# Banded heads of a hybrid attention layer: the half-precision parts of the probabilities are made with queries on partitions and turned by transposing DMAs

## The chip, the cores and the metric

The kernel runs on one core of one Trainium2 chip. The metric is the device time of one execution in microseconds. Before the change it is 1192.52 us, the median of three runs (1192.51 to 1194.84).

## The reference

One decoder layer for one sequence of 2048 tokens and a width of 1024, with two kinds of attention heads side by side. Eight heads of width 64 are "forgetting" heads (causal softmax with a gate bias); eight are banded heads: each query attends to the 128 keys that end at itself, two key heads serve four query heads each, and a learned sink per head enters the softmax's sum only.

```python
h = rms_norm(x, g_pre) * (1 + scale) + shift
qa, ka, va, fa, za, qb, kb, vb, zb = split(h @ w_in)
oa = forgetting_attention(qa, ka, va, fa + b_fgate) * silu(za)
qb, kb = rope(qb), rope(kb)
# banded heads: a block of 128 queries sees its own 128 keys and the block before
s = einsum('bnqhgd,bnshd->bnhgqs', qb, with_prev(kb)) * d ** -0.5
s = where(band & valid, s, -inf)
p = softmax(concat([s, sink]))[..., :-1]
ob = einsum('bnhgqs,bnshd->bnqhgd', p, with_prev(vb)) * silu(zb)
y = concat([oa, ob]) @ w_out
out = x + gate * rms_norm(y, g_post)
```

## The kernel before, in words

Everything is float32 outside. Inside, a product is made of three float16 matmuls: each factor is split into a high part (its value rounded to float16) and a low part (the rest), and high by high, high by low and low by high are summed in PSUM. So wherever a result becomes a factor again, ScalarE (ACT) writes the high part with a copy and VectorE (DVE) the low part with a subtraction.

The program has four stretches: a prologue (modulation, normalisation, the transposed input, the projections of the banded keys and values; up to some 153 us), the banded heads (to some 424 us), the forgetting heads (to some 1020 us) and the output projection. The change lies in the second.

**The banded heads** are 32 windows of class `Pair`: four pairs of heads `j`, and for each the 16 query blocks two by two. One window has two heads and two blocks, so four score tiles of 128 queries by up to 256 keys; the first block of the sequence has no block ahead of it, so four of the 32 windows have six tiles of 128x128 instead of eight. The steps of a window:

- `scores` (L839): twelve matmuls into a PSUM tile `pss`, queries on partitions.
- `maxima` (L852, L856): a fused VectorE instruction per tile adds the band mask, writes the masked scores to `sm_` in SBUF and gives the row maximum; one more makes the bias of the exponential. `sm_` has one extra column per tile for the sink.
- `exps` (L863): four ScalarE exponentials in place in `sm_`, each with its row sum.
- `turn` (L872): TensorE transposes the eight tiles, in float32, into the PSUM tile `pxb`. At the next tick ScalarE copies `pxb` to the high part in `ptb` (L881), at the tick behind it VectorE makes the low part from `pxb` (L877) and the reciprocals of the row sums (L879).
- `pv` (L891): 24 matmuls with keys on partitions; the factors are the tiles of `ptb` and the values `vb`. One tick later VectorE scales the result by the reciprocals into `on` (L897), and a GpSimd DMA stores it (L899).

`sm_`, `ptb`, `pss`, `pxb` and the result `pob` have one buffer each.

**What else runs in this stretch.** TensorE fills the time between these steps with projection units (`fill`): L316 for queries, keys and gates, L334 for values of the forgetting heads, into three PSUM banks `bk`. What follows a unit on the other engines is delayed by ticks. Query projections of the banded heads go through the rotary step: ScalarE copies the bank (L704), four DMAs on SP's queue swap the halves (L706), VectorE multiplies by the cosine (L709), GpSimd by the sine (L719), VectorE adds (L720), ScalarE writes the high part (L721) and VectorE the low part `stb` (L713). Gates have L364, L366 and L356, values L339 and L343. Weights of coming units are loaded, their scale is found on VectorE and GpSimd (L206 to L246), and they are split (L254, L260). Beside it pieces of the output weight are loaded on SP's queue (`wsq`, L1107) and their squares summed on ScalarE (L1103), one piece per window.

**What sets the order.** The instructions of this stretch stand on each engine's queue in the order in which the program emits them (`tc.manual_schedule`), with no scheduler behind it. `tick()` emits what was delayed until then by `after(n, f)`. One window is: a tick; `maxima(n)`; a quarter of the units; a tick; `exps(n)`; a quarter; a tick; a quarter; a tick; a quarter; `pv(n-1)`; `turn(n)`; `scores(n+1)`; the square of piece n-2 and the load of piece n. So the part of `turn` on the other engines is emitted in the window after.

Of the kernel before, what the change touches and what calls it, by code (L numbers as in the profile page):

```python
# [23 lines left out]
CH = 512  # L24
# [16 lines left out]
def hybrid_layer(  # L41
# [17 lines left out]
    V, A, G, PE, SP = nc.vector, nc.scalar, nc.gpsimd, nc.tensor, nc.sync  # L59
# [5 lines left out]
    PSUM = bass.MemoryType.PSUM  # L65
# [14 lines left out]
    def sm(n, tag):  # L80
        return small.tile([P, n], F32, tag=tag, name=tag)
# [60 lines left out]
    ident = const.tile([P, P], F32, name="ident")  # L142
# [258 lines left out]
    def turn(ci, k):  # L401

        px = ps_x.tile([P, CH], F32, tag="x", name="px")
        for u in range(4):
            PE.transpose(px[:, u * P:(u + 1) * P], xt[ci * 4 + u][:, k * P:(k + 1) * P], ident[:])
        hf = hst.tile([P, CH], F32, tag="hf", name="hf")
        hi, lo = hT[ci][:, 0, k, :], hT[ci][:, 1, k, :]

        high = k % 2 == 0 if ci else k in (0, 4)

        def scaled():
            for dst in ([hi] if high else []) + [hf[:]]:
                A.activation(dst, px[:], AF.Identity, scale=Gp[:, k:k + 1], bias=Shp[:, k:k + 1])

        def split():
            if not high:
                V.tensor_copy(hi, hf[:])
            V.tensor_tensor(lo, hf[:], hi, op=ALU.subtract)

        return scaled, split  # L420

    def turn_x(ci, k):
        scaled, split = turn(ci, k)
        after(1, scaled)
        after(2, split)
# [10 lines left out]
    st = start.enter_context(tc.tile_pool(name="start", bufs=1, reuse_waits="tile"))  # L436
    wad = start.enter_context(tc.tile_pool(name="wad", bufs=8, reuse_waits="tile"))
    with tc.manual_schedule():
# [238 lines left out]
    def swa_pool(name, bufs, **kw):  # L677
        return swa.enter_context(tc.tile_pool(name=name, bufs=bufs, reuse_waits="tile", **kw))
# [142 lines left out]
    class Pair:  # L821
# [40 lines left out]
                    p, c = self.sm_[:, e, h, :nk * P + 1], slice(2 * e + h, 2 * e + h + 1)  # L862
                    A.activation(p, p, AF.Exp, bias=self.nb[:, c], accum_out=self.rs[:, c])  # L863

        def turn(self):

            nt = self.nt
            px = ps_t.tile([P, 8, P], F32, tag="t", name="pxb")
            for e, (i, k0, nk) in enumerate(self.blocks):
                for h in range(2):  # L870
                    for b in range(nk):
                        PE.transpose(px[:, self.at[e] + h * nk + b, :], self.sm_[:, e, h, b * P:(b + 1) * P], ident[:])  # L872
            self.ptt = ptp.tile([P, 2, 8, P], F16, tag="pt", name="ptb")
            hi, lo = self.ptt[:, 0, 0:nt, :], self.ptt[:, 1, 0:nt, :]

            def low():
                V.tensor_tensor(lo, px[:, 0:nt, :], hi, op=ALU.subtract)  # L877
                self.rinv = sm(4, "b_ri")
                V.reciprocal(self.rinv[:], self.rs[:])  # L879

            after(1, lambda: A.activation(hi, px[:, 0:nt, :], AF.Copy))  # L881
            after(2, low)

        def pv(self):
# [176 lines left out]
    with swa_order:  # L1061
        fill(N_PRO - 2, tick2)
        psx.close()
        sws = swa_pool("sws", 1)
        ptp = swa_pool("ptp", 1)
        ps_s = swa_pool("ps_s", 1, space=PSUM)
        ps_t = swa_pool("ps_t", 1, space=PSUM)
        ps_pv = swa_pool("ps_pv", 1, space=PSUM)
        wsp = swa_pool("wsp", 3)
        wss, wst = sm(16, "a_m"), sm(2, "wst")  # L1070
        wsq = {}
        base = N_PRO
        NW = len(windows)
        windows[0].scores()
        windows[0].maxima()
        fill(2, tick2)
        windows[0].exps()
        turn_lag[0] = 1
        for n, wd in enumerate(windows):
            goal = base + (N_SWA - base) * (n + 1) // NW  # L1080
            todo = goal - pos[0]
            part = [todo * (m + 1) // 4 - todo * m // 4 for m in range(4)]
            tick()
            if n:
                wd.maxima()
            fill(part[0])
            tick()
            if n:
                wd.exps()
            fill(part[1])  # L1090
            tick()
            fill(part[2])
            tick()
            fill(part[3])
            if n:
                windows[n - 1].pv()
            wd.turn()
            if n + 1 < NW:
                windows[n + 1].scores()

            if n > 1:
                m = n - 2
                A.activation(wsq[m][:], wsq[m][:], AF.Square, accum_out=wss[:, m % 16:m % 16 + 1])  # L1103
            if n == 17:
                V.tensor_reduce(wst[:, 0:1], wss[:], axis=AX.X, op=ALU.add)
            wsq[n] = wsp.tile([P, 2 * P], F32, tag="wsq", name="wsq")
            SP.dma_start(wsq[n][:], w_out0[n // 4 * P:(n // 4 + 1) * P, n % 4 * 2 * P:(n % 4 + 1) * 2 * P])  # L1107
        tick()
        fill(5)
        tick()  # L1110
        fill(5)
        tick()
        fill(6)
        windows[NW - 1].pv()
        tick()
        tick()
        for m in (NW - 2, NW - 1):
# [23 lines left out]
    stp = foxl.enter_context(tc.tile_pool(name="stpa", bufs=3, reuse_waits="tile"))  # L1141
# [117 lines left out]
    class Step:  # L1259
# [28 lines left out]
        def high(self):  # L1288
            self.ph = fxh.tile([P, 2, 2 * CH], F16, tag="ph", name="pha")
            A.activation(self.ph[:, 0, :self.w], self.p32[:, :self.w], AF.Copy)  # L1290
# [199 lines left out]
    with tc.manual_schedule():  # L1490
# [28 lines left out]
        for s, stp_ in enumerate(steps):  # L1519
# [9 lines left out]
            a = b = 0  # L1529
# [91 lines left out]
```

## Time and profile before

| | us |
|---|---|
| median of three runs | 1192.52 |
| the profiled execution | 1193.52 |
| its span, first to last instruction | 1191.8 |
| its mean granted TensorE clock | 0.989 of full |

Busy time of the engines by stretch of the span, in us (PE is TensorE, PEld its weight loads):

| stretch | length | PE | PEld | DVE | ACT | POOL | clock |
|---|---|---|---|---|---|---|---|
| 0 to 153 | 153 | 133.71 | 77.06 | 100.56 | 86.47 | 21.28 | 0.98 |
| 156 to 424 (banded heads) | 268 | 267.82 | 191.01 | 194.51 | 148.75 | 76.83 | 1.00 |
| 426 to 1020 (forgetting heads) | 594 | 581.28 | 329.91 | 489.86 | 387.99 | 73.66 | 0.99 |
| 1020 to 1191 | 171 | 161.03 | 81.77 | 114.24 | 49.73 | 0.00 | 0.99 |

Rows of the profile read as follows. A group of instructions shows line, engine, operation and tile names (output first), partitions by elements and type, how many; behind the bar the busy us of the group, the mean ns of one, and the idle us of the engine just before them with what ended most of it. A row of the waits shows who waited for whom, the total us, how often, and the longest. A row of one line's times shows minimum, median and maximum ns and when it ran. A row of the timeline begins with the start and the duration in us; a bracket at its end is a wait just before it and its releaser.

### The profile page before, as it was taken

What the parts mean: (1) busy time and instruction counts of PE and PEld (TensorE: products, weight loads), DVE (VectorE), ACT (ScalarE), POOL (GpSimd) and SP (SyncE); (2) the same over time, 40 slices, a digit from 0 to 9 for tenths busy, and PEclk for the clock granted to TensorE, in tenths of its full rate; (3) what the DMA queues carried; (4) which work ended last, traced back from release to release, by engine and by line L of the source; (5) the groups of instructions that cost most, each with busy time, mean ns of one, the idle gap of its engine ahead of it and who ended that gap; (6) DMA issues with size and microseconds to landing.
All of it is one profiled execution on the core that took longest, in us unless ns stands there. A gap on an engine that the chain in (4) does not pass through costs nothing. (4 is left out here: it accounts for less than half of the span.)

```text
span 1191.8 us, 27330 instructions
## 1 busy us (share of the span) xinstructions
PE 1147.6 (96%) x10738; PEld 681.5 (57%) x10738; DVE 901.6 (76%) x2295; ACT 675.0 (57%) x1118; POOL 173.3 (15%) x311
## 2 busy tenths in 40 slices
PE   5899999999999999999999999999999979999996
PEld 1466567655569956555555555555555555555553
DVE  6776567777777737888988898888877897767665
ACT  4676445555555542666666676676756778333331
POOL 1001223232331311012111101111000100000000
PEclk9999999999999999999999999999999979999999
DMA  9645333233322222143223232131111145455652
GB/s 331 209 138 164 84 76 72 78 91 93 87 81 66 69 61 70 39 105 75 77 65 85 60 72 68 44 80 37 44 43 37 59 142 169 147 184 170 209 170 81
DMA packets 88725, 120.12 MB, mean 101 GB/s; under 512 B 27772, under 2 KB 64676, under 8 KB 88596
## 3 DMA queue, kind: packets, MB, share of 16 engines
q1 hardware_dynamic: 77636, 86.20, 24.9%
q0 software_dynamic: 10624, 31.91, 10.4%
q8 instruction: 84, 1.38, 0.5%
q14 instruction: 45, 0.37, 0.1%
q10 hardware_dynamic: 336, 0.26, 0.1%
HBM read 70.97 MB, written 25.18 MB: 81 GB/s over the span
## 5 line engine op out<-in xcount | busy, mean ns | idle before, releaser
L1282 ACT ACTIVATE p<-sta,lift,scl_qk 128x1024 f32<-128x1024 f32 (+2 forms) x160 | 171.9, 1074 | 115.2 <-PE sta L1278 103.0
L316 PE MATMUL bk<-hT,wh_qk 128*128 128x512 f16 x768 | 194.6, 378 | 0.0
L1428 PE MATMUL bk<-wohl,oz 128*128 128x512 f16 x768 | 172.4, 379 | 2.0 <-ACT wohl L1368 0.8
L1293 DVE TENSOR_TENSOR pha<-p,pha 128x1024 f16<-128x1024 f32 (+2 forms) x160 | 169.4, 1059 | 0.2 <-ACT pha L1290 0.2
L1290 ACT ACTIVATE pha<-p 128x1024 f16<-128x1024 f32 (+2 forms) x160 | 148.1, 926 | 36.2 <-POOL p L1286 30.4
L1231 DVE TENSOR_REDUCE a_m<-bk 128x1 f32<-128x512 f32 x192 | 129.5, 684 | 44.1 <-PE bk L1228 43.8
L1428 PEld LDWEIGHTS <-oz 128*128 128x128 f16 x768 | 74.4, 99 | 84.0 <-issue 1.8
L1303 PE MATMUL poa<-vt,pha 128*128 128x65 f16 x1088 | 118.3, 194 | 3.6 <-DVE ona L1312 3.6
L1306 PE MATMUL poa<-vt,pha 128*128 128x65 f16 x1088 | 117.7, 193 | 1.7 <-DVE pha L1293 1.6
L1305 PE MATMUL poa<-vt,pha 128*128 128x64 f16 x1088 | 118.2, 195 | 0.0
L1277 PE MATMUL sta<-T 128*128 128x512 f16 (+1 forms) x320 | 110.8, 351 | 5.6 <-ACT p L1282 5.5
L316 PEld LDWEIGHTS <-wh_qk 128*128 128x128 f16 x768 | 72.4, 97 | 74.8 <-issue 0.8
L1303 PEld LDWEIGHTS <-pha 128*128 128x128 f16 x1088 | 102.7, 97 | 18.3 <-DVE ona L1312 4.8
L1228 PE MATMUL bk<-T 66*128 66x512 f16 (+2 forms) x320 | 109.8, 350 | 0.1
L1305 PEld LDWEIGHTS <-pha 128*128 128x128 f16 x1088 | 102.0, 98 | 13.6 <-issue 0.3
L1278 PE MATMUL sta<-T 69*128 69x512 f16 (+1 forms) x320 | 109.3, 352 | 0.0
L1306 PEld LDWEIGHTS <-pha 128*128 128x128 f16 x1088 | 101.8, 99 | 2.2 <-DVE pha L1293 2.2
L316 PE MATMUL bk<-hT,wh_za 128*128 128x512 f16 x384 | 99.8, 378 | 0.0
L1286 POOL TENSOR_SCALAR_AFFINE_SELECT p<-p 128x256 f32<-128x256 f32 x64 | 33.0, 516 | 439.5 <-ACT p L1282 434.8
L334 PE MATMUL bk<-wh_va,hT 128*128 128x128 f16 x1536 | 91.2, 219 | 0.0
L334 PEld LDWEIGHTS <-hT 128*128 128x128 f16 x1536 | 87.5, 98 | 5.4 <-issue 2.6
L316 PE MATMUL bk<-hT,wh_zb 128*128 128x512 f16 x384 | 89.8, 379 | 0.0
(494 smaller groups left out, 1908.6 us busy)
## 6 DMA issues: line engine op xcount, KB each, us to landing
wa<-in_w_ada_dram SPq DMA_DIRECT2D x16, 512.0 KB
z_d<-tz POOLq DMA_DIRECT2D x32, 256.0 KB, 2.7
T<-stq SPq DMA_DIRECT2D x128, 64.0 KB
T<-o_d SPq DMA_DIRECT2D x16, 512.0 KB
T<-z_d SPq DMA_DIRECT2D x16, 512.0 KB
xr<-in_x_dram SPq DMA_DIRECT2D x16, 512.0 KB
out_dram<-yg SPq DMA_DIRECT2D x15, 512.0 KB
xt<-in_x_dram SPq DMA_DIRECT2D x12, 512.0 KB
```

What stands on the lines that cost most here:

```text
L316: PE.matmul(ps, whl[:, a, k, :], hT[ci][:, b, k, :], start=(k == 0 and n == 0), stop=(k == KT - 1 and n == 2))
L334: PE.matmul(ps[:, u * P:(u + 1) * P], hT[ci][:, a, k, u * P:(u + 1) * P], whl[:, b, k, :], start=(k == 0 and n == 0), stop=(k == KT - 1 an ...
L1228: PE.matmul(mx[:, :w], T[0:XM, 0, i * P:(i + 1) * P], T[0:XM, 2, pc * CH:pc * CH + w], start=True, stop=True)
L1231: V.tensor_reduce(m3[:, u, pc:pc + 1], mx[:, :w], axis=AX.X, op=ALU.max)
L1277: PE.matmul(self.st[:, o:o + w], T[:, 3, kb_], T[:, 1, qc], start=True, stop=False)
L1282: A.activation(self.p32[:, :self.w], self.st[:, :self.w], AF.Exp, scale=scl[f"qk{self.hd}"][:], bias=lift[:])
L1290: A.activation(self.ph[:, 0, :self.w], self.p32[:, :self.w], AF.Copy)
L1293: V.tensor_tensor(self.ph[:, 1, :self.w], self.p32[:, :self.w], self.ph[:, 0, :self.w], op=ALU.subtract)
L1303: PE.matmul(po[:, u, :], ph[:, 0, pq], vt[:, b, hd, 0:65], start=(self.first and n == 0 and u == 0), stop=False)
L1305: PE.matmul(po[:, u, 0:64], ph[:, 0, pq], vt[:, b, hd, 65:VW], start=False, stop=False)
L1306: PE.matmul(po[:, u, :], ph[:, 1, pq], vt[:, b, hd, 0:65], start=False, stop=(self.last and n == len(self.blocks) - 1))
L1428: PE.matmul(py, self.hl[:, i, k, :], w_slot(8 * j + k)[:, cc], start=(k == 0 and m_ == 0), stop=(k == KT - 1 and m_ == 2))
```

## The change

`turn` is replaced by `split`. It is emitted right behind the window's own `exps`. One tick after that ScalarE copies the probabilities from `sm_` as they lie (queries on partitions) to a float16 staging tile `sp0` (L880), and a DMA on SP's queue turns its eight 128x128 tiles into the high part of `ptb` (`dma_start_transpose`, L881). At the tick behind that VectorE makes the low part from `sm_` and `sp0` in a second staging tile `sp1` (L885), which a second such DMA turns into `ptb` (L886); the reciprocals follow as before (L888). The staging tiles come from the pool `stp`, which has two buffers under the tag "st". Windows with blocks of unequal width take two instructions per part. TensorE's transposes and the PSUM pool of `pxb` are gone, `ptb` has two buffers, `wsq` has one of its own with every odd piece in a buffer that `cm` used, and each square of a piece is emitted one window earlier. Behind the change P.V is L900, its scaling L906, the square L1112 and the load of `wsq` L1117; lines further on stand ten later.

```diff
-        def turn(self):
-            nt = self.nt
-            px = ps_t.tile([P, 8, P], F32, tag="t", name="pxb")
-            for e, (i, k0, nk) in enumerate(self.blocks):
-                for h in range(2):
-                    for b in range(nk):
-                        PE.transpose(px[:, self.at[e] + h * nk + b, :], self.sm_[:, e, h, b * P:(b + 1) * P], ident[:])
+        def split(self):
+            n = self.nt * P
+            part = [stp.tile([P, 2, CH], F16, tag="st", name=f"sp{a}")[:].rearrange("p a c -> p (a c)")
+                    for a in range(2)]
             self.ptt = ptp.tile([P, 2, 8, P], F16, tag="pt", name="ptb")
-            hi, lo = self.ptt[:, 0, 0:nt, :], self.ptt[:, 1, 0:nt, :]
+            if self.blocks[0][2] == self.blocks[1][2]:
+                cuts = [(self.sm_[:].rearrange("p e h c -> p (e h) c")[:, :, 0:2 * P], 0, 4)]
+            else:
+                cuts = [(self.sm_[:, e, :, 0:b[2] * P], self.at[e], 2) for e, b in enumerate(self.blocks)]
...
+            def high():
+                for p, (hi, lo) in cuts:
+                    A.activation(hi, p, AF.Copy)
+                SP.dma_start_transpose(self.ptt[:, 0, 0:self.nt, :], part[0][:, 0:n])
 
             def low():
-                V.tensor_tensor(lo, px[:, 0:nt, :], hi, op=ALU.subtract)
+                for p, (hi, lo) in cuts:
+                    V.tensor_tensor(lo, p, hi, op=ALU.subtract)
+                SP.dma_start_transpose(self.ptt[:, 1, 0:self.nt, :], part[1][:, 0:n])
                 self.rinv = sm(4, "b_ri")
                 V.reciprocal(self.rinv[:], self.rs[:])
 
-            after(1, lambda: A.activation(hi, px[:, 0:nt, :], AF.Copy))
+            after(1, high)
             after(2, low)
...
-        ptp = swa_pool("ptp", 1)
+        ptp = swa_pool("ptp", 2)
-        ps_t = swa_pool("ps_t", 1, space=PSUM)
-        wsp = swa_pool("wsp", 3)
+        wsp = swa_pool("wsp", 1)
...
             if n:
                 wd.exps()
+                wd.split()
...
                 windows[n - 1].pv()
-            wd.turn()
             if n + 1 < NW:
                 windows[n + 1].scores()
-            if n > 1:
-                m = n - 2
+            if n:
+                m = n - 1
```

On VectorE, one window in the middle, from the bias of its exponentials (L856) to the scaling of a P.V (L897, now L906). `ptb` is the turned probabilities, `sp_` a staging tile, `sm__` the probabilities, `bk` a projection's bank. Before:

```order
L856 TENSOR_SCALAR b_nb<-b_m 128x4
L343 SCALAR_TENSOR_TENSOR vt<-bk_137,vt 128x4x64 x2
L877 TENSOR_TENSOR ptb<-pxb,ptb 128x1024
L879 RECIPROCAL b_ri<-b_rs 128x4
L720 TENSOR_TENSOR qc<-qc,qs 128x512
L211 TENSOR_REDUCE wmx<-wr_zb_2432 128x1
L213 STREAM_TRANSPOSE wmt_112<-wmx 128x32
L713 TENSOR_TENSOR stb<-qc,stb 128x512
L709 SCALAR_TENSOR_TENSOR qc<-bk_136,cosT 128x512
L897 TENSOR_TENSOR on<-pob,b_ri 128x256
```

With the change:

```order
L856 TENSOR_SCALAR b_nb<-b_m 128x4
L343 SCALAR_TENSOR_TENSOR vt<-bk_137,vt 128x4x64 x2
L720 TENSOR_TENSOR qc<-qc,qs 128x512
L885 TENSOR_TENSOR sp_2530<-sm__2505,sp_2529 128x1024
L888 RECIPROCAL b_ri<-b_rs 128x4
L211 TENSOR_REDUCE wmx<-wr_zb_2424 128x1
L213 STREAM_TRANSPOSE wmt_112<-wmx 128x32
L713 TENSOR_TENSOR stb<-qc,stb 128x512
L709 SCALAR_TENSOR_TENSOR qc<-bk_136,cosT 128x512
L906 TENSOR_TENSOR on<-pob,b_ri 128x256
```

The low part stood behind L856 and was that of the window before; now it is that of the same window, reads `sm__`, and stands behind one more rotary step (L720), with the weight's maximum (L211), two rotary steps (L713, L709) and the scaling of the window before behind it.

On ScalarE, from the exponentials of one window to those of the next. Before:

```order
L863 ACTIVATE sm__3231,b_rs<-sm__3231,b_nb 128x257 x4
L366 ACTIVATE tz<-bk_137,cz_zb_3057 128x512
L1103 ACTIVATE wsq,a_m<-wsq 128x256
L881 ACTIVATE ptb<-pxb 128x1024
L721 ACTIVATE stb<-qc 128x512
L863 ACTIVATE sm__3340,b_rs<-sm__3340,b_nb 128x257 x4
```

With the change:

```order
L863 ACTIVATE sm__3514,b_rs<-sm__3514,b_nb 128x257 x4
L880 ACTIVATE sp_3545<-sm__3514 128x1024
L1112 ACTIVATE wsq,a_m<-wsq 128x256
L366 ACTIVATE tz<-bk_136,cz_zb_3033 128x512
L863 ACTIVATE sm__3621,b_rs<-sm__3621,b_nb 128x257 x4
```

The copy to the high part (L881, now L880) stood before the exponentials of the next window and read PSUM; now it stands right behind those of its own window, in `sm__`, and the square of a piece of the output weight behind it.

On SP's queue, around a rotary step's four DMAs (L706). Before:

```order
L1107 DMA wsq<-in_w_out_dram 128x256 x2
L706 DMA qs<-qf 32x512 x4
L1107 DMA wsq<-in_w_out_dram 128x256 x2
L706 DMA qs<-qf 32x512 x4
L1107 DMA wsq<-in_w_out_dram 128x256 x7
```

With the change:

```order
L1117 DMA wsq<-in_w_out_dram 128x256
L881 DMA_TRANSPOSE ptb<-sp_3108 128x6x128
L706 DMA qs<-qf 32x512 x4
L886 DMA_TRANSPOSE ptb<-sp_3109 128x6x128
L1117 DMA wsq<-in_w_out_dram 128x256
L881 DMA_TRANSPOSE ptb<-sp_3216 128x8x128
L886 DMA_TRANSPOSE ptb<-sp_3217 128x8x128
L1117 DMA wsq<-in_w_out_dram 128x256
```

Between two loads of `wsq` there now stand the two transposing DMAs of a window, and in some windows the four L706 between those two.

More of the change, by code (lines that the diff above doesn't have):

```diff
@@ L863, in exps @@
                     A.activation(p, p, AF.Exp, bias=self.nb[:, c], accum_out=self.rs[:, c])
-        def turn(self):
-            nt = self.nt
-            px = ps_t.tile([P, 8, P], F32, tag="t", name="pxb")
-            for e, (i, k0, nk) in enumerate(self.blocks):
-                for h in range(2):
-                    for b in range(nk):
-                        PE.transpose(px[:, self.at[e] + h * nk + b, :], self.sm_[:, e, h, b * P:(b + 1) * P], ident[:])
-            self.ptt = ptp.tile([P, 2, 8, P], F16, tag="pt", name="ptb")
-            hi, lo = self.ptt[:, 0, 0:nt, :], self.ptt[:, 1, 0:nt, :]
+        def split(self):
+            n = self.nt * P
+            part = [stp.tile([P, 2, CH], F16, tag="st", name=f"sp{a}")[:].rearrange("p a c -> p (a c)")
+                    for a in range(2)]
+            self.ptt = ptp.tile([P, 2, 8, P], F16, tag="pt", name="ptb")
+            if self.blocks[0][2] == self.blocks[1][2]:
+                cuts = [(self.sm_[:].rearrange("p e h c -> p (e h) c")[:, :, 0:2 * P], 0, 4)]
+            else:
+                cuts = [(self.sm_[:, e, :, 0:b[2] * P], self.at[e], 2) for e, b in enumerate(self.blocks)]
+            cuts = [(p, [t[:, at * P:at * P + k * p.shape[2]].rearrange("p (k c) -> p k c", k=k) for t in part])
+                    for p, at, k in cuts]
+            def high():
+                for p, (hi, lo) in cuts:
+                    A.activation(hi, p, AF.Copy)
+                SP.dma_start_transpose(self.ptt[:, 0, 0:self.nt, :], part[0][:, 0:n])
             def low():
-                V.tensor_tensor(lo, px[:, 0:nt, :], hi, op=ALU.subtract)
+                for p, (hi, lo) in cuts:
+                    V.tensor_tensor(lo, p, hi, op=ALU.subtract)
+                SP.dma_start_transpose(self.ptt[:, 1, 0:self.nt, :], part[1][:, 0:n])
                 self.rinv = sm(4, "b_ri")
                 V.reciprocal(self.rinv[:], self.rs[:])
-            after(1, lambda: A.activation(hi, px[:, 0:nt, :], AF.Copy))
+            after(1, high)
             after(2, low)
@@ L1077, in hybrid_layer @@
         windows[0].exps()
+        windows[0].split()
         turn_lag[0] = 1
@@ L1096, in hybrid_layer @@
                 windows[n - 1].pv()
-            wd.turn()
             if n + 1 < NW:
                 windows[n + 1].scores()
-            if n > 1:
-                m = n - 2
+            if n:
+                m = n - 1
                 A.activation(wsq[m][:], wsq[m][:], AF.Square, accum_out=wss[:, m % 16:m % 16 + 1])
-            if n == 17:
+            if n == 16:
                 V.tensor_reduce(wst[:, 0:1], wss[:], axis=AX.X, op=ALU.add)
-            wsq[n] = wsp.tile([P, 2 * P], F32, tag="wsq", name="wsq")
+            wsq[n] = (fap.tile([P, 2 * P], F32, tag="cm", name="wsq") if n % 2 else
+                      wsp.tile([P, 2 * P], F32, tag="wsq", name="wsq"))
             SP.dma_start(wsq[n][:], w_out0[n // 4 * P:(n // 4 + 1) * P, n % 4 * 2 * P:(n % 4 + 1) * 2 * P])
@@ L1116, in hybrid_layer @@
         tick()
-        for m in (NW - 2, NW - 1):
+        for m in (NW - 1,):
             A.activation(wsq[m][:], wsq[m][:], AF.Square, accum_out=wss[:, m % 16:m % 16 + 1])
```

## The prediction

> **What bounds the kernel now.** I read the granted clock first (0.989, one core), then the busy time by stage, then the waits, then one pair of blocks in order of time. The banded heads run from the first of their score matmuls (156.3 us) to the last (404.5 us), 31 steps from one pair to the next. The columns behind the length are the busy time of PE, PEld, DVE, ACT and POOL with instruction counts, then granted clock, DMA share and GB/s.
>
> ```profile
> 156.30:404.50 248.20, 248.02 (x2895) 171.71 (x2896) 183.26 (x535) 140.91 (x394) 72.19 (x140) 1.00 0.30 79
> ```
>
> The waits of PE, from 168 to 411 us, hold a single row:
>
> ```profile
> PE pob L891 <- DVE ptb L877: 0.2, 1, 0.2
> ```
>
> TensorE is busy in 248.02 of 248.20 us at full clock and waits 0.2 us: this stage is its own queue, 248.2/31 = 8.01 us a step. VectorE has 183.26 us of work, 5.9 us a step. This looks like a stage in which whatever leaves TensorE is won, so the question is what stands 0.9 us behind it. One step, from the scores of a pair to those of the next:
>
> ```profile
> 300.02 0.83 PE L839 MATMUL pss<-kst,stb 64*128 64x256 f16 x12
> 300.89 0.54 DVE L852 CUSTOM_DVE_ANT_0 sm__4253<-pss,bmask,snk 128x256 f32<-128x256 f32 x1
> 301.36 0.54 DVE L852 CUSTOM_DVE_ANT_0 sm__4253<-pss,bmask,snk 128x256 f32<-128x256 f32 x1
> ...
> 302.88 0.19 DVE L856 TENSOR_SCALAR b_nb<-b_m 128x4 f32<-128x4 f32 x1
> 303.16 0.51 ACT L863 ACTIVATE sm__4253<-sm__4253,b_nb 128x257 f32<-128x257 f32 x1 [1.95 <-DVE b_nb L856]
> 304.22 1.21 DVE L877 TENSOR_TENSOR ptb<-pxb,ptb 128x1024 f16<-128x1024 f32 x1
> 305.06 0.19 ACT L863 ACTIVATION_READ_ACCUMULATOR sm__4253<-sm__4253,b_nb 128x1 f32 x1
> ...
> 306.87 0.42 DVE L897 TENSOR_TENSOR on<-pob,b_ri 128x256 f32<-128x256 f32 x1 [0.34 <-PE pob L891]
> 307.67 0.83 PE L839 MATMUL pss<-kst,stb 64*128 64x256 f16 x12
> ```
>
> Two things are to be seen. A pair's masking with its row maxima (L852 to L856) ends 2.18 us after it starts, at 303.07; its exponentials end at 305.25. And the low half that VectorE makes at 304.22 (L877) is that of the pair before, from PSUM, while ScalarE does this pair's exponentials: today the split lies beside them.
>
> **The change part by part. TensorE loses 248 transposes.** Busy time of L872 alone, PE and then PEld:
>
> ```profile
> 160.00:413.00 253.00, 33.35 (x248) 26.68 (x248) 1.00 0.29 77
> ```
>
> Weight loads follow each other without a gap, so 26.68 us is their pace (0.108 us each; eight for most pairs, six for four of them), and matmul spans overlap. The 0.17 us of issue that the timeline shows ahead of L839 I leave, since L316 behind L839 has the like (0.21): it goes with the change from 128 rows to 64, not with the transpose. **Term 1: -26.7 us**; a step of TensorE becomes 8.01 - 0.86 = 7.15 us.
>
> **The split moves into the circle of one pair.** The tile of scores and probabilities has one buffer. Its next maxima stand on VectorE behind the low half, which reads that tile, and the low half needs ScalarE's high half, which needs the exponentials. So from one pair's maxima to the next pair's there now lie in series: maxima, exponentials, high half, low half, the reciprocal, and the output scaling of an earlier pair (L897). The halves from SBUF have the same shape as those of the forgetting heads (minimum/median/maximum ns):
>
> ```profile
> L1290 ACT ACTIVATE pha<-p x160: 510/1044/1058, 465.8 to 1018.7; 128x1024 f16<-128x1024 f32 x96, 128x896 f16<-128x896 f32 x32, 128x384 f16<-128x384 f32 x32
> L1293 DVE TENSOR_TENSOR pha<-p,pha x160: 546/1214/1240, 472.0 to 1023.0; 128x1024 f16<-128x1024 f32 x96, 128x896 f16<-128x896 f32 x32, 128x384 f16<-128x384 f32 x32
> ```
>
> They cost what L881 and L877 cost now, so neither engine does more; what is new is that VectorE must stand still for 3.2 us of ScalarE. The bare circle: 2.18 + 2.18 (303.07 to 305.25) + 1.04 + 1.21 + 0.09 + 0.42 = 7.1 us; with the 0.08 by which a VectorE instruction starts before the last one's end (300.89 to 301.36 for a row of 0.54) taken off behind the low half and the scaling, 7.0. With such an overlap taken off everywhere, on ScalarE too, 6.55. TensorE's step is 7.15: the bare circle just fits. But other work stands in it: in the new order, over the 31 steps, VectorE has between a low half and the next maxima 7 of L709, 6 of L713, 4 of L356, 3 each of L211, L260 and L720, 10 of L343 and three weight scalings of about 0.5 us (L239 to L246); ScalarE has 4 of L721 and 3 of L254 between exponentials and high half.
>
> ```profile
> L709 DVE SCALAR_TENSOR_TENSOR qc<-bk,cosT 128x512 f32<-128x512 f32 x14 | 9.6, 683 | 0.0
> L720 DVE TENSOR_TENSOR qc<-qc,qs 128x512 f32<-128x512 f32 x14 | 9.5, 681 | 1.6 <-POOL qs L719 1.3
> L713 DVE TENSOR_TENSOR stb<-qc,stb 128x512 f16<-128x512 f32 x14 | 9.5, 678 | 4.2 <-ACT stb L721 4.2
> L343 DVE SCALAR_TENSOR_TENSOR vt<-bk,vt 128x256 f16<-128x256 f32 x22 | 8.2, 415 | 2.0 <-ACT vt L339 2.0
> L356 DVE SCALAR_TENSOR_TENSOR tz<-tz,bk 128x512 f32<-128x512 f32 x8 | 5.4, 676 | 4.0 <-ACT tz L366 4.0
> L260 DVE SCALAR_TENSOR_TENSOR wh_qb<-wr_qb,w_sw,wh_qb 128x512 f16<-128x512 f32 x6 | 4.4, 737 | 1.5 <-ACT wh_qb L254 1.5
> L211 DVE TENSOR_REDUCE wmx<-wr_va 128x1 f32<-128x1024 f32 x3 | 3.6, 1193 | 0.0
> L254 ACT ACTIVATE wh_va<-wr_va,w_sw 128x1024 f16<-128x1024 f32 x3 | 3.4, 1141 | 1.3 <-DVE w_sw L246 1.3
> L721 ACT ACTIVATE stb<-qc 128x512 f16<-128x512 f32 x14 | 8.7, 621 | 6.2 <-DVE qc L720 6.2
> ```
>
> Each taken 0.08 to 0.1 short, that is 7x0.60 + 6x0.60 + 4x0.60 + 3x(1.11 + 0.66 + 0.60) + 10x0.33 + 3x0.5 + small ones 0.9 = 23 us on VectorE and 4x0.53 + 3x1.04 = 5.2 on ScalarE: 28 us, in 19 of the 31 steps and up to 3.8 in one. The other 12 steps cannot make it up, because scores and probabilities have one buffer each. Of the 28, 0.15 us of spare in each of 19 steps (2.9) and two short pairs (1.7) go off: +23. With the circle of 6.55 the spare is 0.6, and +15 is left. I take +21, nearer the end that the timeline shows. **Term 2: +21 (+15 to +23).**
>
> **The transposing DMAs.** No DMA of this kind is in the trace. Two a pair, 256 KB each, on SP's queue. The nearest rows (KB each, median us to landing; then issue times of SP):
>
> ```profile
> z_d<-tz POOLq DMA_DIRECT2D x8, 256.0 KB, 2.7
> wr_va<-in_w_in_dram POOLq DMA_DIRECT2D x3, 512.0 KB, 5.3
> L706 SPq DMA_DIRECT2D qs<-qf x80: 507/583/1349, 53.9 to 363.5; - x80
> ```
>
> The row nearest in bytes and source is 2.7 us, that in many small pieces 5.3: I take 3.5. Room: scores of a pair end at 300.85, its P.V starts two steps on less one P.V and one set of scores (about 1.9 us), 12.4 us later; maxima to low half use 6.7; so 5.7 us are left for the low half's DMA, less whatever stands in that pair's circle. In three steps the four L706 stand on SP between the two DMAs, 4x0.58 = 2.3 us; there, and where 3 us of other work stood in the circle, P.V waits 1 us or so. Behind that wait stand the next scores and all projections on TensorE. **Term 3: +3 (0 to +8).** The loads of wsq have a step of 7 us where they had two or three; they are half as large as z_d's 256 KB. **0.**
>
> **The clock.** Term 2 arrives as waits of TensorE, some of 2 to 3 us. Later in this trace (one row for each stretch, PE only, then clock; and TensorE's waits from 955 to 985 us, total, times, longest):
>
> ```profile
> 955.00:961.80 6.80, 4.63 (x49) 1.00 0.34 97
> 961.80:968.60 6.80, 5.08 (x53) 0.50 0.37 104
> 968.60:975.50 6.90, 4.80 (x57) 0.99 1.00 288
> 975.50:982.30 6.80, 6.24 (x42) 0.50 0.36 110
> PE sta L1277 <- ACT p L1282: 4.2, 3, 2.7
> PE poa L1303 <- DVE ona L1312: 2.3, 2, 1.9
> ```
>
> After stretches with 2 us idle the clock was 0.50 for 6.8 us, half of which is lost: 3.4 us. I count one such stretch, **term 4: +3.4 (0 to +10)**. [...]
>
> **Sum:** -26.7 + 21 + 3 + 3.4 = +0.7 us on the profiled execution (1193.52 around a span of 1191.8). That one lay 1.0 above the median of the runs, 1192.52; so 1193.2.
>
> **Rivals.** *The whole gain arrives:* if the projections' VectorE work slips into the 3.2 us in which VectorE waits, TensorE stays the bound: 1192.5 - 26.7 = 1165.8. For it: VectorE's 183 us are far below TensorE's new 221.5. Against it: the queue is in order, and the listed work stands behind the low half.
>
> *The transposing DMA is slow:* from 5.7 us on, each microsecond more delays P.V in all 31 steps, and ScalarE's next high half too, which waits for its staging buffer. At 6.5 us: 31x0.8 = 25 us on top of term 2, 1218. For it: 512 KB in pieces of 512 B took 5.3. Against it: both sides are SBUF, and the 16 DMA engines are only 0.30 busy here. [...]
>
> **How the numbers follow.** Circle as the bound, terms 2 to 4 as above: 0.70, 1193.2, own range 1185 to 1202 (term 2 at +15 without terms 3 and 4 gives 1181; with all at their upper ends 1207). Whole gain 0.10. Slow DMA 0.20. About 0.2%, or 2.4 us, is what a measurement tells from no change. Of the 0.70, 0.19 lie under 1190.1, 0.31 within, 0.20 above 1194.9. Faster 0.10 + 0.19 = 0.29, same 0.31, slower 0.20 + 0.20 = 0.40. The range leaves out the whole gain and half of the slow DMA: 1181 (term 2 at its lower end, terms 3 and 4 at nothing) to 1212.
>
> **What would show it.** Right: no L872; TensorE in the stage busy some 220 us with 20 or more of idle, put down to P.V (waiting for a DMA or the low half) or to scores waiting for VectorE; VectorE idle ahead of the low half, released by the high half; perhaps a stretch at half clock. Wrong: the stage at 221 us with TensorE gapless (the circle does not bind, or ends sooner than I add it up), or transposing DMAs of 5 us and more.

## The result, and the profile after

The changed kernel takes 1200.93 us (median of four runs, 1200.55 to 1202.71) against 1192.51 us before. The ratio is 1.0069, 95% interval 1.0051 to 1.0086: it is slower, by 6 to 10 us.

All of it is in the banded heads. From the first score matmuls to the last the stage took 248.20 us before; after, the same columns (length, busy time of PE, PEld, DVE, ACT and POOL, granted clock, DMA share, GB/s) read:

```profile
155.50:411.40 255.90, 230.37 (x2657) 151.69 (x2658) 184.68 (x539) 141.21 (x398) 72.23 (x139) 0.97 0.67 136
```

The stage is 7.7 us longer; what lies around it is 943.0 us of the span (1198.9 - 255.9) against 943.6 before (1191.8 - 248.2). TensorE was without a gap before; now it idles for 25.53 us, and its 230.37 us of busy time are 9.03 more than 248.02 - 26.68 = 221.34, what the work that is left takes at full clock. So TensorE's own account of the stage is: less transposes, plus idle time (0.18 before), plus extra busy time, -26.68 + 25.35 + 9.03 = +7.70. It says how TensorE spent the stage, not what made the stage longer.

The longest waits of TensorE in the stage of the changed kernel (us in total, times, longest):

```profile
PE pob L900 <- DMA ptb<-sp: 19.8, 15, 6.6
PE pob L900 <- DVE on L906: 2.7, 2, 2.2
PE bk L334 <- DVE wh_va L260: 1.3, 1, 1.3
PE pss L839 <- DVE b_m L852: 1.1, 2, 0.7
```

Read alone, this says that P.V waits for the transposing DMAs. The waits of VectorE there tell something else; here are the three longest, and all that it waits for TensorE:

```profile
DVE sp L885 <- ACT sp L880: 36.1, 25, 3.3
DVE sp L885 <- DMA ptb<-sp: 10.7, 3, 5.6
DVE stb L713 <- ACT stb L721: 8.1, 4, 2.3
DVE sm__3621 L852 <- PE pss L839: 0.4, 1, 0.4
DVE sm__3727 L852 <- PE pss L839: 0.2, 1, 0.2
```

VectorE stands still for 36.1 us for the high half, 25 times, with the next row maxima behind it (37.3 us where the expectations below count from 150 to 430 us). For TensorE's scores it waits 0.6 us in the whole stage: TensorE waits for VectorE's queue, hardly the other way round. The worst place, and ahead of it an ordinary pair and a wait of another kind, in the timeline of the changed kernel (start, duration):

```profile
204.93 1.27 SPq L886 DMA_TRANSPOSE ptb<-sp  x1
208.11 0.81 PE L900 MATMUL pob<-vb,ptb 128*128 128x64 f16 x22 [1.01 <-DMA ptb<-sp]
...
225.70 0.86 PE L900 MATMUL pob<-vb,ptb 128*128 128x64 f16 x24 [2.15 <-DVE on L906]
...
248.11 1.23 DVE L885 TENSOR_TENSOR sp<-sm__3299,sp 128x1024 f16<-128x1024 f32 x1 [0.20 <-ACT sp L880]
249.51 2.55 SPq L706 DMA_DIRECT2D qs<-qf  x4
252.17 1.30 SPq L886 DMA_TRANSPOSE ptb<-sp  x1
252.25 0.90 POOL L206 DMA_DIRECT2D wr_zb<-in_w_in_dram  x1
259.02 1.35 PE L900 MATMUL pob<-vb,ptb 128*128 128x64 f16 x22 [6.59 <-DMA ptb<-sp]
259.07 1.23 DVE L885 TENSOR_TENSOR sp<-sm__3407,sp 128x1024 f16<-128x1024 f32 x1 [5.64 <-DMA ptb<-sp]
```

The ordinary low half lands 3.2 us after its DMA is issued (204.93 to 208.11). At 252.17 the low half's DMA was issued 2.8 us after the subtraction had ended, behind the four L706; a weight load of 512 KB started 0.08 us behind it and landed after 6.7 us; the low half landed after 6.85 us. P.V waited for that low half, and so did the next low half, which writes the same staging tile. Two more low halves landed late, after 7.3 us (277.08 to 284.40) and 5.2 us (351.54 to 356.74), each with such a load under way.

The granted clock was half of full in three stretches of the stage. The rows are the stretch ahead of the first, the first, the stretch ahead of the second, the second, and the third (length, PE busy, clock, DMA share, GB/s):

```profile
224.00:227.40 3.40, 0.97 (x26) 1.00 0.47 97
227.40:230.80 3.40, 3.40 (x18) 0.51 0.37 58
251.30:254.70 3.40, 0.80 (x5) 1.00 0.74 159
254.70:264.90 10.20, 5.88 (x42) 0.50 0.80 175
357.10:360.50 3.40, 3.40 (x45) 0.51 0.48 144
```

They hold 3.40 + 5.88 + 3.40 = 12.7 us of TensorE's busy time, so the lower clock accounts for some 6.3 of the 9.0 us of extra busy time. The other 2.7 us came at full clock; what makes them was not tested.

### The profile page after: what moved, and what is told of

Read it like the earlier page. It is cut to its first block, busy times and chain, and to the rows that moved or that the text cites. A ratio compares the mean times of both kernels' runs of the same rounds, so it can differ in the third digit from the quotient of the medians.

```text
span 1198.9 us, 26963 instructions
## 1 busy us (share of the span) xinstructions
PE 1127.7 (94%) x10490; PEld 660.2 (55%) x10490; DVE 903.8 (75%) x2299; ACT 675.3 (56%) x1122; POOL 173.7 (14%) x311
```

## The experiments

The table sums up the banded stage of each run's profile, one execution each: its length from first to last scores, TensorE's idle time in it, and as "extra" TensorE's busy time beyond what its work takes at full clock (221.3 us; 224.8 where transposes are left, 247.3 with the filler). The lower clock is a part of "extra", not all of it: with the low half on GpSimd and P.V later the granted clock was 1.00 in the whole stage. Where P.V comes later, the stage holds one P.V less (24 matmuls, under 0.9 us). Behind these columns stand the median of all executions and the ratio to the kernel before on the same chip.

| | stage | idle | extra | median | ratio (95%) |
|---|---|---|---|---|---|
| before | 248.2 | 0.2 | 0 | 1192.5 | |
| the change | 255.9 | 25.5 | 9.0 | 1200.9 | 1.0069 (1.0051 to 1.0086) |
| one transpose per pair, old order | 227.3 | 1.9 | 0.7 | 1172.3 | 0.9825 (0.9808 to 0.9841) |
| no transposing DMAs | 250.2 | 22.8 | 6.1 | 1194.6 | 1.0010 (1.0000 to 1.0019) |
| P.V half a step later | 254.3 | 24.7 | 8.3 | 1194.2 | 1.0019 (1.0000 to 1.0037) |
| second buffer alone | 252.0 | 23.6 | 7.0 | 1196.8 | 1.0032 (1.0020 to 1.0044) |
| low half behind the next maxima | 276.4 | 38.5 | 16.6 | 1219.8 | 1.0228 (1.0210 to 1.0247) |
| the same, P.V half a step later | 228.0 | 6.8 | 0 | 1172.4 | 0.9822 (0.9807 to 0.9836) |
| the same, P.V later still | 225.9 | 4.6 | 0 | 1171.4 | 0.9814 (0.9798 to 0.9831) |
| low half on GpSimd | 252.5 | 20.2 | 11.0 | 1194.8 | 1.0014 (1.0003 to 1.0024) |
| the same, P.V half a step later | 238.0 | 15.3 | 1.4 | 1185.2 | 0.9936 (0.9919 to 0.9954) |
| L706 on GpSimd's queue | 263.1 | 29.8 | 12.0 | 1208.1 | 1.0128 (1.0111 to 1.0146) |
| filler on TensorE | 263.3 | 11.5 | 4.5 | 1206.1 | 1.0106 (1.0089 to 1.0123) |

**What the transposes are worth by themselves.** The kernel before, one transpose per pair:

```diff
-            for e, (i, k0, nk) in enumerate(self.blocks):
-                for h in range(2):
-                    for b in range(nk):
-                        PE.transpose(px[:, self.at[e] + h * nk + b, :], self.sm_[:, e, h, b * P:(b + 1) * P], ident[:])
+            PE.transpose(px[:, 0, :], self.sm_[:, 1, 1, 0:P], ident[:])
+            px = px[:, 0:1, :].broadcast_to([P, nt, P])
```

> The kernel before with one transpose per pair in place of eight (six in four pairs), read eight times by both halves (the output is another one): TensorE loses 216 of 248 transposes, 0.108 us each, and no order is changed. If the whole of that arrives, -23.2 us: 1169. If something stands close behind TensorE in the old order too (VectorE 5.9 us a step, the one PSUM tile of the turned probabilities), less: 1175 to 1188.

The stage of this kernel:

```profile
155.70:383.00 227.30, 225.45 (x2686) 150.32 (x2687) 182.09 (x535) 139.16 (x391) 71.75 (x139) 1.00 0.32 87
```

It is 20.9 us shorter, of the 23.2 us of transposes taken away, at full clock and with 1.9 us of idle. Nearly the whole gain arrives in the old order. So nothing stood within 0.67 us a step (20.9/31) behind TensorE before the change; what holds the changed kernel came with it.

**The change without its DMAs.**

```diff
-            part = [stp.tile([P, 2, CH], F16, tag="st", name=f"sp{a}")[:].rearrange("p a c -> p (a c)")
-                    for a in range(2)]
             self.ptt = ptp.tile([P, 2, 8, P], F16, tag="pt", name="ptb")
+            part = [self.ptt[:, a].rearrange("p a c -> p (a c)") for a in range(2)]
...
-                SP.dma_start_transpose(self.ptt[:, 0, 0:self.nt, :], part[0][:, 0:n])
...
-                SP.dma_start_transpose(self.ptt[:, 1, 0:self.nt, :], part[1][:, 0:n])
```

> The change without its transposing DMAs: both halves are written straight into ptb, so P.V multiplies probabilities that were not turned (the output is another one); everything else stands as in the change. Two theories of the 25 us that TensorE idles and the 9 us that the lower clock takes in the banded stage (255.9 us from first to last scores; the rest of the execution is 944.7). Circle: VectorE's series sets the pace (184.7 us of work, 37.3 us of standing still for the high halves, some 24 us of other waits, 246 in all), and the DMAs only add to it: stage 236 to 246, total 1181 to 1191, TensorE waits for low halves and scores. DMA: the landing time of the DMAs (3 to 7 us after their issue) and their load make the waits: without them TensorE is the bound again, stage 221 to 227, total 1166 to 1172.

Its stage, the two longest waits of TensorE in it, and the longest of VectorE (here L897 is P.V, L903 its scaling, L879 the high and L883 the low half):

```profile
155.70:405.90 250.20, 227.41 (x2657) 150.54 (x2658) 184.79 (x530) 137.52 (x391) 71.85 (x138) 0.99 0.29 78
```

```profile
PE pss L839 <- DVE b_m L852: 10.6, 15, 1.0
PE pob L897 <- DVE on L903: 6.3, 8, 2.5
DVE ptb L883 <- ACT ptb L879: 41.4, 27, 3.3
```

The circle, by 4 us more than its expectation: without any turning the stage is still 2 us longer than before, and TensorE still idles for 22.8 us. Only the name of what it waits for has changed, from the DMA to VectorE. VectorE waits for TensorE nowhere in this stage, and ScalarE once, for 0.8 us: VectorE and ScalarE set the pace between them. The DMAs cost the difference to the change, 5.7 us of the stage: 2.7 of TensorE's idle time and 3.0 of its extra busy time. Two steps of VectorE show the circle, a bare one (260.38 to 267.36) and, above it, one with work in it:

```profile
215.92 0.54 DVE L852 CUSTOM_DVE_ANT_0 sm__2904<-pss,bmask,snk 128x256 f32<-128x256 f32 x1
221.31 0.75 DVE L260 SCALAR_TENSOR_TENSOR wh_zb<-wr_zb,w_sw,wh_zb 128x512 f16<-128x512 f32 x1 [3.24 <-ACT wh_zb L254]
222.25 1.23 DVE L883 TENSOR_TENSOR ptb<-sm__2904,ptb 128x1024 f16<-128x1024 f32 x1 [0.20 <-ACT ptb L879]
224.12 1.21 DVE L211 TENSOR_REDUCE wmx<-wr_qb 128x1 f32<-128x1024 f32 x1
226.79 0.40 DVE L852 CUSTOM_DVE_ANT_0 sm__3054<-pss,bmask,snk 128x128 f32<-128x128 f32 x1
...
260.38 0.54 DVE L852 CUSTOM_DVE_ANT_0 sm__3466<-pss,bmask,snk 128x256 f32<-128x256 f32 x1
262.44 1.21 DVE L211 TENSOR_REDUCE wmx<-wr_zb 128x1 f32<-128x1024 f32 x1
265.82 1.23 DVE L883 TENSOR_TENSOR ptb<-sm__3466,ptb 128x1024 f16<-128x1024 f32 x1 [0.75 <-ACT ptb L879]
267.36 0.53 DVE L852 CUSTOM_DVE_ANT_0 sm__3569<-pss,bmask,snk 128x256 f32<-128x256 f32 x1
```

The bare step takes 6.98 us. In it L211 and some rotary work cost nothing: they stand ahead of the low half, in time that VectorE would wait out. In the upper step the same L211 stands behind the low half, ScalarE's L254 between exponentials and high half, and the step takes 10.87 us.

**P.V later.** In this edit and those that use it, P.V is emitted behind the exponentials of the second pair after it:

```diff
             if n:
                 wd.exps()
+            if n > 1:
+                windows[n - 2].pv()
+            if n:
                 wd.split()
...
-            if n:
-                windows[n - 1].pv()
```

> The change with P.V of each pair emitted half a step (some 3.6 us) later, behind the exponentials of the second pair after it; nothing else moved. DMA: the 19.8 us in which P.V waits for landings and the clock's 9 us go, stage 222 to 230, total 1167 to 1175. Circle: VectorE keeps its pace, TensorE's waits move from P.V to the scores (for the row maxima) or to a projection's bank; only VectorE's own 10.7 us behind slow landings can shrink: stage 242 to 256, total 1187 to 1201.

```profile
PE pob L900 <- DMA ptb<-sp: 12.4, 10, 3.6
PE pss L839 <- DVE b_m L852: 9.7, 8, 3.6
```

As the circle had it: the waits move from P.V to the scores, and VectorE keeps its pace. (The profiled execution was the slowest of seven, 1199.58; the median, 1194.19, is 0.5% under the change.)

**Two buffers, and the low half behind the next maxima.** The room for a second `sm_` came from the buffer of the even `wsq` pieces (they are loaded in two halves into tiles no longer used), one query tile and one tile of weight maxima. First the second buffer with nothing moved:

```diff
-        sws = swa_pool("sws", 1)
+        sws = swa_pool("sws", 2)
...
-        wsp = swa_pool("wsp", 1)
...
-        abp = swa_pool("abp", 4)
+        abp = swa_pool("abp", 3)
```

> The second buffer for scores and probabilities and the room made for it (as in the run with the low half behind the next row maxima), but every instruction in the place that the change gives it. If the one buffer closed the circle, the next row maxima need no longer wait and most of the gain is there: 1172 to 1182. If VectorE's order closes it (the low half waits for ScalarE at the head of VectorE's queue, with the next row maxima behind it, whatever the buffers), nothing: 1196 to 1203, VectorE standing still for high halves some 35 us as in the change. It is also the control for the smaller pools.

```profile
DVE sp L885 <- ACT sp L880: 35.0, 26, 3.3
```

VectorE stands as long as in the change. It is the order of its queue that closes the circle; the buffer alone, with the smaller pools, gives some 4 us. Then the order, with P.V later as above:

```diff
-            after(2, low)
+            self.low = low
...
             if n:
                 wd.maxima()
+                windows[n - 1].low()
```

> Scores and probabilities get a second buffer and the low half moves on VectorE behind the row maxima of the next pair, so VectorE has work while ScalarE makes exponentials and high half; P.V half a step later as in the run before. For the room the odd pieces of the output weight keep their buffer, the even ones come in two halves, and query tiles have three buffers instead of four, weight maxima two instead of three. Circle: VectorE's 37 us of standing still are filled, its 185 us of work and 24 us of other waits fit under TensorE's 221: stage 221 to 232, total 1166 to 1177. DMA: the low half and P.V move together, the room between them is what it was in the change, the waits stay: stage 245 to 256, total 1190 to 1201.

```profile
154.80:382.80 228.00, 221.25 (x2633) 144.37 (x2634) 183.57 (x538) 144.78 (x428) 71.97 (x138) 1.00 0.73 151
```

```profile
PE pob L900 <- DMA ptb<-sp: 6.6, 7, 1.2
```

TensorE's work is 221.25 us at full clock, the circle is open, and the stage is 20.2 us shorter than before the change; 1172.4 us beats both kernels. The same two transposing DMAs per pair run here, at a DMA share of 0.73, so their landing and their load do not hold the stage by themselves. With P.V where the change has it:

> The low half behind the next row maxima with the second buffer, but P.V in the place that the change gives it, so the low half's DMA has some 3.6 us less until P.V. If the order on VectorE is what counts, most of the gain stays and P.V waits more for landings than the 6.6 us with the later P.V, some 0.5 us a step: 1175 to 1188. If the later P.V was the other half of the gain, the waits come back as in the change: 1190 to 1201.

1219.8: this missed the first expectation by 32 us and the second by 19, and P.V waits 38.4 us for landings, 22 times. One step in the timeline of that kernel:

```profile
277.66 1.23 DVE L885 TENSOR_TENSOR sp<-sm__3525,sp 128x1024 f16<-128x1024 f32 x1
278.91 1.25 SPq L886 DMA_TRANSPOSE ptb<-sp  x1
282.37 0.81 PE L900 MATMUL pob<-vb,ptb 128*128 128x64 f16 x22 [0.82 <-DMA ptb<-sp]
283.22 0.42 DVE L906 TENSOR_TENSOR on<-pob,b_ri 128x256 f32<-128x256 f32 x1 [2.47 <-PE pob L900]
283.99 0.54 DVE L852 CUSTOM_DVE_ANT_0 sm__3741<-pss,bmask,snk 128x256 f32<-128x256 f32 x1 [0.34 <-PE pss L839]
286.05 1.23 DVE L885 TENSOR_TENSOR sp<-sm__3634,sp 128x1024 f16<-128x1024 f32 x1
```

The step shows a second circle, through P.V: low half, landing of its DMA (3.5 us after the issue), P.V, its scaling on VectorE, scores, maxima, the next low half: 8.39 us. The low half was moved nearer to P.V, and the DMA came into the round. So the theory became two circles, of which opening one is not enough.

**The low half on another engine.** The run with the second buffer, and GpSimd for the subtraction:

```diff
-                    V.tensor_tensor(lo, p, hi, op=ALU.subtract)
+                    G.tensor_tensor(lo, p, hi, op=ALU.subtract)
```

> The change with the second buffer (as in its run alone, 1.0032 of before) and the low half's subtraction on GpSimd in place of VectorE, P.V where the change has it. VectorE stands for ScalarE's high half no more; GpSimd does (its 128x512 product took 1.27 us, so 128x1024 some 2.5 us; its own circle: sink column 0.3, exponentials 2.2, high half 1.0, low half 2.5, store and other issues 0.7 to 1.3, 6.7 to 7.3 us a step). If an engine standing in its queue is the cause: stage 226 to 240, 1171 to 1185. If the lateness of the low half and its DMA is all that counts, 1.3 us later each: 1196 to 1210.

The median lies between both expectations, at 1194.8. GpSimd, then TensorE, wait:

```profile
POOL sp L885 <- ACT sp L880: 57.9, 20, 5.1
```

```profile
PE pob L900 <- DMA ptb<-sp: 20.0, 15, 4.1
```

VectorE no longer stands for the high half, yet P.V waits as in the change: the circle through P.V is still closed. With P.V later besides:

> The run with the low half on GpSimd and the second buffer, and P.V half a step later besides. Two circles are now the theory: one through VectorE's queue (row maxima, ScalarE's two steps, low half, next maxima), one through P.V (scores, maxima, exponentials, both halves, the DMA's landing, P.V, and its scaling on VectorE ahead of later maxima). Opening one alone gave 1194 (P.V later) and 1195 (low half off VectorE); opening both with VectorE's own order gave 1172. If that holds whatever engine makes the low half, opening both here too gives most of it: stage 226 to 238, total 1171 to 1183. If the gain of that run came from the low half's place alone, and GpSimd's standing for the high half (57.9 us in the run without the later P.V) takes VectorE's part, nothing: 1190 to 1197.

```profile
PE pob L900 <- DMA ptb<-sp: 9.0, 9, 2.5
```

1185.2: 2 us beyond the first expectation, well below the second. Opening both circles gives a gain with this engine too, less than with VectorE's reordered queue. Where the 13 us between the two medians come from was not isolated.

**The rotary step's DMAs off SP's queue.**

```diff
-                    SP.dma_start(qs[32 * r:32 * r + 32, :], qf[32 * (r ^ 1):32 * (r ^ 1) + 32, :])
+                    (SP if pool else G).dma_start(qs[32 * r:32 * r + 32, :], qf[32 * (r ^ 1):32 * (r ^ 1) + 32, :])
```

> The change with the four DMAs of each rotary step (L706) issued by GpSimd instead of SyncE, so that none stands on SP's queue between the DMA of a high half and that of its low half; all else as in the change. The low half of the longest wait (6.6 us, 252.4 to 259.0) was issued 2.9 us after its subtraction had ended, behind four of them; in all some five pairs have them there. If SP's queue is what makes the waits: 10 to 15 us less, 1186 to 1191. If VectorE's circle is, only what the DMAs add (5.7 us in the stage) can shrink: 1194 to 1201.

It was slower than either theory allowed, 1208.1. Waits on GpSimd, and on ScalarE for GpSimd:

```profile
POOL qs L706 <- ACT qf L704: 40.4, 9, 6.0
```

```profile
ACT sm__4392 L863 <- POOL sm__4392 L850: 5.1, 1, 5.1
```

GpSimd's queue now stands for ScalarE's copy L704, and behind it the copy of the sink column (L850), without which an exponential cannot start. ScalarE's exponentials wait for that copy eight times between 155 and 419 us, against once in the change (5.7 us). VectorE stood 42.9 us for high halves, 6.8 more than in the change. That this lengthening of the circle is the whole of the 7 us is argued, not shown. Since the edit loaded GpSimd's queue as well, the run does not show what SP's queue alone is worth.

**Work given back to TensorE.**

```diff
             if n:
+                for _ in range(4):
+                    PE.matmul(idle[:], identh[:], hT[0][:, 0, 0, :], start=True, stop=True)
                 windows[n - 1].pv()
```

> The change with four matmuls of 128x512 per pair ahead of P.V, on data that lies there, into a PSUM tile that nobody reads (the rest of the computation is whole): TensorE gets back 31 times 4 times 0.216 us, 26.8 us, about what the transposes took. If TensorE's queue still set the pace of the banded stage, 1200.9 + 26.8 = 1228. If VectorE's circle does, the filler runs where TensorE idled (25 us) and the total stays: 1198 to 1206; with shorter idle stretches the clock should stay up more, so TensorE's busy time beyond filler and work should fall from 9 us to 0 to 5, and the total may come out a few us lower, 1194 to 1198.

```profile
156.20:419.50 263.30, 251.77 (x2777) 161.87 (x2778) 187.37 (x541) 142.68 (x400) 72.31 (x139) 0.98 0.67 132
```

The filler that falls into the stage (30 of the 31 times; four matmuls took 1.03 us in the timeline and one 0.38, which puts them about 0.216 us apart: 25.9 us) costs 7.4 us there and about 0.4% of the time, not 27 us, at the upper end of what the circle let expect. TensorE is not the bound in the change. Its idle time fell from 25.5 to 11.5 us and its extra busy time from 9.0 to 4.5.

**P.V later still.** Last, on the best version, P.V goes behind the second quarter of the units, with the turned tile allotted in the high half:

```diff
             fill(part[1])
+            if n > 1:
+                windows[n - 2].pv()
             tick()
```

> The low half behind the next row maxima, and P.V a further quarter of a step (1.8 us) later, the turned tiles allotted with the high half. The 6.6 us in which P.V still waits for landings (7 waits, 1.2 us at most) should go: stage 222 to 225, total 1165 to 1170. If the next high half's DMA now waits for this P.V, whose buffer it takes, and comes late in turn, no gain: 1171 to 1176.

The stage is 2.1 us shorter in the profile, and P.V waits 3.8 us for landings instead of 6.6. But the median, 1171.4, lies in the second expectation, and the two intervals (0.9798 to 0.9831, 0.9807 to 0.9836) overlap: the same within what was measured, about 1.8% under the kernel before. Whether the reason is the one expected was not examined.

## Why the prediction was right or wrong

The main mechanism is right: the case that was called likeliest, VectorE's circle as the new bound, is what happened, and its own range, 1185 to 1202, holds 1200.9. The sum is too small: it came out at +0.7 us, no change, and the result is +8.4. That the time still lies in the stated range owes something to its width, 31 us. Point by point:

- **Term 1, -26.7, held.** In the run with the low half behind the next maxima and P.V later, TensorE's busy time in the stage is 221.25 us at full clock (with one P.V less) where 221.3 are expected, and in the old order 20.9 of 23.2 us arrived.
- **The bare circle, 7.0 us, held:** 6.98 in five steps of the run without DMAs. The other work in it is what the prediction named, L211 and the rotary step behind the low half, L254 ahead of the high half.
- **Term 2, +21, was too small, with term 4.** By TensorE's idle time it looks right: 22.8 - 0.2 = 22.6 us in the run without DMAs. But the length of that stage is what the circle takes, and it is 250.2 us, where the sum without term 3 gives 248.2 - 26.7 + 21 + 3.4 = 245.9 (242.5 without the clock). As neither VectorE nor ScalarE waits for TensorE there but once, for 0.8 us, these 4.3 us or more lie in the circle itself. What makes them was not isolated. The sum had left out VectorE's waits for GpSimd's sine product (L720 for L719, 3.4 us over two) and eight instances of L856 that took longer than in the step it went by (5.2 us together; last section).
- **Term 3, +3, was too small within its range:** the DMAs cost 5.7 us of the stage. The landing was put at 3.5 us; an ordinary one took 3.2. The DMA at 252.17, behind four L706, is the place that was named, at 1 us; P.V waited 6.6 us there. 4.3 and 2.7 us make up the 7.0 between +0.7 and +7.7.
- **Term 4, the clock,** was sized by one stretch at half clock, +3.4 us. There were three, and they put 6.3 us on TensorE's busy time. The sum added this to the circle as if TensorE's pace still counted. How much of it lengthened the stage is not shown: VectorE waited for TensorE's scores 0.6 us in all, ScalarE for its banks 10.4 us in seven waits, and ahead of two of the three stretches P.V waited for a late low half, ahead of the first for VectorE's scaling.
- **The rival of a slow DMA** (from 5.7 us on): the sign named for it, DMAs of 5 us and more, was seen in three pairs (6.85, 7.3 and 5.2 us), each beside a weight load. As a rule it is false: the other low halves that P.V waited for landed in 2.8 to 4.9 us, and the best version runs the same DMAs.
- **The rival of the whole gain** is false for the change and true for its reordering: 0.9814 and 0.9822 are what it gave, with 20 to 22 us less in the stage.
- **What the signs would be.** VectorE idle ahead of the low half, released by the high half: there. TensorE with 20 us or more of idle: 25.5. Most of that idle time, 19.8 us, is put down to P.V waiting for a DMA; this row would have led a reader to the DMA, and the run without DMAs shows that for most of it this is a label for lateness, not its cause.
- **Not seen:** the second circle, through P.V, the DMA and the scaling on VectorE. The prediction took P.V's place as a room of 5.7 us that is used up now and then. It decides the reordering: against the kernel before, the reordering costs 27 us without the later P.V and gains 21 with it.

On the clock: ahead of the fall at 227.4 TensorE worked for 0.97 of the 3.40 us before it, and its longest wait there was 2.15 us; at 254.7 the clock fell when the wait of 6.6 us had lasted 2.3. On SP's queue the issue of a transposing DMA took 1.2 to 1.3 us for most:

```profile
L881 SPq DMA_TRANSPOSE ptb<-sp x32: 1221/1242/2472, 161.3 to 418.4; - x32
L886 SPq DMA_TRANSPOSE ptb<-sp x32: 1212/1283/3744, 165.2 to 419.7; - x32
```

## What to carry to other kernels

When work leaves the engine that sets the pace, write down the next circle with its engines' order, not their busy time. In the change VectorE waited at the low half for 36.1 us, 25 times, and the next row maxima, behind it in the queue, waited with it. In the run without DMAs L211 ahead of the low half was free (6.98 us a step), while the step with L211 behind it and L254 ahead of the high half took 10.87 us. To open such a circle, put the waiting instruction behind work that is ready, and move its consumer away by as much: both together took the stage from 248.2 to 228.0 us, the consumer alone left it at 254.3 and the waiting instruction alone at 276.4, where the change has 255.9. And a row that says "waits for the DMA" names what came last; take the DMA away before you believe it (19.8 us were put down to the DMA here, and TensorE idled for 22.8 us without it).

## What the runs showed of the hardware

- In the changed kernel a transposing DMA of 256 KB from SBUF to SBUF occupied SP's queue for 1.24 us (median of L881; 1.28 of L886, the longest 3.74; a rotary DMA of 64 KB: 0.59). It landed 3.2 us after its issue in an ordinary pair and 5.2 to 7.3 us after it in three pairs with a weight load of 512 KB under way (issued at 252.25, 275.31 and 354.57). With the two per pair the DMA share of the stage was 0.67, against 0.30 before and 0.29 in the run without them.
- In the changed kernel TensorE's granted clock was 0.50 to 0.51 for 3.4 us (10.2 us once) after stretches of 3.4 us in which TensorE had idled for 2.2 to 2.6 us (busy 0.97, 0.80 and, from 353.7 to 357.1, 1.15 us), in no case the whole stretch.
- VectorE's L856, 0.17 us as a rule, took 1.47 us in the run without DMAs while GpSimd's product L719 ran, and ended with it (332.50 against 332.46). Rows of VectorE and of GpSimd in that run:

```profile
331.03 1.47 DVE L856 TENSOR_SCALAR b_nb<-b_m 128x4 f32<-128x4 f32 x1
```

```profile
331.18 1.28 POOL L719 TENSOR_TENSOR qs<-qs,sinT 128x512 f32<-128x512 f32 x1
```

Seven more of its 32 instances took 0.67 to 0.86 us, each with L719 beside it. They stand in the circle; what makes them long was not tested.
